# Two operand tiles moved by 160 bytes in SBUF, the tiles behind them by 512

## The chip, the cores and the metric

The kernel runs on one core of one Trainium2 chip. The metric is device time of one execution in microseconds. Engines are named as in the profile: PE is TensorE (PEld its weight loads), DVE is VectorE, ACT is ScalarE, POOL is GpSimd, SP is SyncE, from whose queue all DMAs of the kernel are issued.

## The reference

A network of three layers on 512 tokens of width 1024, in float32. Layers 0 and 1 are attention blocks (stick-breaking attention, then dilated attention), layer 2 mixes a gated linear recurrence of four heads with differential attention of four heads and is modulated by a vector computed from a condition c. Each layer ends in a gated feed-forward network of width 2816:

```python
u = rmsnorm(h, norm2_w[l]) * (1.0 + sc2) + sh2
ff = (jax.nn.silu(u @ w_ffn_gate[l]) * (u @ w_ffn_up[l])) @ w_ffn_down[l]
h = h + g2 * ff
```

Nearly all the arithmetic is products of the token matrix with weight matrices: queries, keys and values, the output products, and gate, up and down of the feed-forward networks.

## The kernel before

**Layout.** Tokens lie along the free axis, features on the 128 partitions. h, the running state, is one tile of 8 k-tiles by 512 tokens. A product needs float32 accuracy out of float32r matmuls, so each operand is split in two: xh is the operand rounded to float32r and xl the rest, both of the shape of h (ACT writes xh in `split_hi`, DVE writes xl in `split_lo`, or `out_operand` does both for the attention's output o). Weights are split the same way into whi (ACT) and wlo (DVE).

**The trio.** One 128x128 weight tile costs three matmuls of 512 columns, `mm3`: xh by whi, xl by whi, xh by wlo. The moving operand is x, the stationary one the weight tile.

```python
def mm3(o, w, x, first, last, n=T):
    E.mm(o, w[0], x[0], first, False, n=n)
    E.mm(o, w[0], x[1], False, False, n=n)
    E.mm(o, w[1], x[0], False, last, n=n)
```

`gemm_a` runs 8 k-tiles of one output tile, 24 matmuls into one PSUM bank. `gemm_wide` runs several output tiles side by side. `out_proj` runs the attention output's product in two parts. In `vcols` (the values of layer 2) the roles are turned: 128 tokens of xh or xl are stationary and four weight tiles move, whi,xh and its like in the profile. `ffn` makes the gate and up products from xh and xl, with 22 column tiles each; its two halves write the activations to eleven tiles ph0 to ph10 and their rests to pl0 to pl10, and the down product runs the same trio on these, 33 matmuls for an output tile. In the last layer the gate and up products of the first three column tiles run in two halves of 256 tokens, and so do the first tiles of the input product and the end of an output product.

**The weight stream.** The host packs all weights in the order of use (`weight_plan`). A unit of 16 tiles, 1 MB, is loaded into one of two buffers wraw; each half of it, 8 tiles, is split into one of three whi and wlo buffers of 1024 columns.

**What sets the order.** The helper class `Core` records each instruction with a planned clock for each engine; threads wait for planned times and flags, and the order of every engine's list follows from it, once, when the program is built. Addresses play no part in it.

**SBUF.** Persistent tiles are taken first, in the order h, xh, xl, vt, cr (masks and the identity), ones, eps, mod, sc, acc, acc2, rb, rc, gv (lines 395 to 408). Behind them come the pool of the weight buffers, small work tiles, and a pool for each phase. Each tile starts at a multiple of 32 bytes. In each partition they start at:

```
tile          first byte    remainder by 512    remainder by 2048
h                  16512                 128                  128
xh                 32896                 128                  128
xl                 49280                 128                  128
cr                 67264                 192                 1728
wraw               76064                 288                  288
whi (3)     92448 + 4096                 288                  288
wlo (3)    104736 + 4096                 288                  288
ph0 to ph10       129312                 288                  288
pl0 to pl10       151840                 288                  288
```

A k-tile of xh or xl, and each of the ph and pl, is 2048 bytes; a weight tile is 512 bytes, so the weight tiles of a buffer take four places by 2048.

Of the kernel before, what the change touches and what calls it, by code (L numbers as in the profile page):

```python
# [10 lines left out]
FT = mybir.dt.float32  # L11
# [6 lines left out]
P = 128  # L18
# [7 lines left out]
EPS = 1e-6  # L26
# [120 lines left out]
class Pool:  # L147
    """A tile pool that knows when the slot of a new tile is free."""
# [13 lines left out]
class Core:  # L162
    """Emission helpers. A clock per engine and the times at which data are there order the
    instructions of the threads that a phase consists of: a thread yields the time, the flag or
    the condition it waits for."""
# [24 lines left out]
    def inherit(self, name, old):  # L190
        """The tile takes over the slot of an older one."""
        t = [max(w, r) for _, _, w, r, _, _ in self.spans.pop(old, [])]
        if t:
            self.spans[name] = [(0, 1 << 30, 0.0, max(t), None, None)]
# [26 lines left out]
    def _run(self, eng, cost, outs, ins):  # L221
        """The time at which an instruction ends, and when others may use what it made."""
        t = max(getattr(self, eng), self._ready(eng, outs, ins)) + cost
        setattr(self, eng, t)
        self._done(eng, outs, ins, t + LAT)
        return t + LAT
# [69 lines left out]
    def dma(self, out, a, kb, sbuf=False):  # L296
        """sbuf: the source lies on chip."""
        self.nc.sync.dma_start(out, a)  # L298
        t = max(self.dma_t, self._ready("dma_t", [out], [a] if sbuf else []) + 1.4, self.pe_t + 1.4) + kb / 360.0
        self.dma_t = t  # L300
        self._done("dma_t", [out], [a] if sbuf else [], t + DMALAT)
        return t + DMALAT
# [4 lines left out]
    def there(self, *aps):  # L307
        """Waits until the tensor engine may use these."""
        t = self._ready("pe_t", (), aps)
        if t > self.pe_t:  # L310
            yield t

    def clear(self, *aps):
        """Waits until the tensor engine may write these."""
        t = self._ready("pe_t", aps, ())
        while t > self.pe_t:
            yield t
            t = self._ready("pe_t", aps, ())
# [22 lines left out]
    def reserve(self, banks):  # L341
        """Takes these banks out of the pool, the ones in use when they are released."""
        self.held = [b for b in banks if b not in self.free]
        self.free = [b for b in self.free if b not in banks]
# [9 lines left out]
    def run(self, main):  # L354
        """Threads run when what they wait for is there, by priority; main fills in between."""
        self.spawn(main, 1000)
        live = self.threads
        while live:
            ready = []
            for th in live:  # L360
                c = th[3]
                if c is None or (c in self.flags if isinstance(c, str) else c()):
                    ready.append(th)
            assert ready, ([(th[0], th[3]) for th in live], self.free)
            now = [th for th in ready if th[4] <= self.pe_t]
            if now:
                th = min(now, key=lambda q: (q[0], q[1]))
            else:
                th = min(ready, key=lambda q: q[4])
                self.pe_t = th[4]  # L370
            th[3], th[4] = None, 0.0
            try:
                r = next(th[2])
            except StopIteration:
                live.remove(th)
                continue
            if isinstance(r, (int, float)):
                th[4] = r
            else:
                th[3] = r  # L380
# [3 lines left out]
def kernel(ctx: ExitStack, tc, wst, wada, xT, vec, cst, rope, bias1, alibi, hmask, out):  # L384
# [10 lines left out]
    h = persist.tile([P, KT, T], FT, name="h")  # L395
    xh = persist.tile([P, KT, T], FR, name="xh")
# [11 lines left out]
    gv = persist.tile([P, 64], FT, name="gv")  # L408

# [33 lines left out]
    def finish(hu):  # L443
        """Splits a half where the engines have nothing else to do."""
        hs, ls = highs[hu], lows[hu]
        while hs or ls:
            if quiet:
                yield lambda: not quiet
                continue
            th = max(E.act_t - SLACK, E._ready("act_t", [hs[0][0]], [hs[0][1]])) if hs else 1e9  # L450
            tl = max(E.dve_t - SLACKD, ls[0][0]) if ls else 1e9
            if min(th, tl) > E.pe_t:
                yield min(th, tl)
            elif th <= E.pe_t:
                raise_(hu)
            else:
                lower(hu)

        load_ahead()
# [9 lines left out]
    def load_ahead():  # L469
        """The next unit takes the place of one whose halves are split."""  # L470
        while state["loaded"] < NUNITS:
            old = 2 * (state["loaded"] - RAWBUFS)
            if any(x >= state["prepped"] or highs[x] or lows[x] for x in range(max(old, 0), old + 2)):
                break
            load_unit()
# [79 lines left out]
    def gemm_wide(banks, i0, hook=None, need=None, wide=False, halves=None):  # L555
        """Several m-tiles side by side, while the operand is still being made; wide: their weights alternate."""
# [41 lines left out]
    def update(m, bank, tag, x=True, gain=None, scale=None, gain2=None, after=None, t=None):  # L598
        """h[m] += psum, its squares, and (x) the next product's operand; t is the half of the tokens."""
# [63 lines left out]
    def col_sums(src, bank, tbs=ALL, c0=0, first=True, s0=0):  # L663
        """Sums over the partitions; the first ones into a bank come with first set."""
        for tb in tbs:
            E.mm(ps[:, bank, c0 + tb:c0 + tb + 1], src[:, tb * P - s0:(tb + 1) * P - s0], ones, first, True, n=16,
                 group=False)
            first = False

    def newton(dst, y, m, n):  # L670
        """dst = y (1.5 - m y^2 / 2)."""
        t = tmp.tile([P, 2, n], FT, name="nw", bufs=4)
        E.stt(t[:, 0], y, -0.5, m, OP.mult, OP.mult, n=4)
        E.tt(t[:, 1], t[:, 0], y, OP.mult, n=4)
        return E.stt(dst, t[:, 1], 1.5, y, OP.add, OP.mult, n=4)
# [7 lines left out]
    def rstd_bank(dst, bank, width, tbs=ALL):  # L683
        """dst = (sums / width + EPS)^-1/2."""
# [19 lines left out]
    def norm(tag, cols, banks=None, table=None, gate=None):  # L704
        """rc and rb from acc."""
# [26 lines left out]
    def zv(g, hd, c0, c1):  # L732
        """Columns of a head's scores: two heads share the bank of group 1."""
        if g == 1:
            return ps[:, 2, hd * 256 + c0:hd * 256 + c1]
        return ps[:, ZB[g][hd], c0:c1]
# [6 lines left out]
    def make_pad(pool):  # L743
        """The stationary operands of group 1 span all rows, so that its heads may share a bank."""
# [10 lines left out]
    def split_two(t, lo, src, scale):  # L755
        """The high parts of two heads, each on its rows of t[:, hd], and the low parts."""
# [9 lines left out]
    def stacked(pool, name, src, bufs=1, scale=1.0):  # L766
        """The stationary operand of two heads: a head's high part on its rows, its low part on the others."""
# [4 lines left out]
    def doubled(pool, name, src, bufs=1, scale=1.0):  # L772
        """The moving operand of two heads: a head's high part on both halves of the rows; and the low parts."""
# [10 lines left out]
    def place(t, src, other):  # L784
        """Each head's rows of src to its own rows of t[:, hd] or to the others."""
# [20 lines left out]
    def out_operand(tag, o, flags, xfree, order=tuple(range(KT))):  # L806
        """The operand of out_proj takes the place of the phase's own, k-tile by k-tile."""
# [8 lines left out]
    def out_proj(tag, upd, order=tuple(range(KT)), scale=None, halves=None):  # L816
        """h += o @ w, in two parts: the k-tiles that come first, and the last ones."""
# [120 lines left out]
    def evac_v(tag, pool, p, bank, vz, keep=False):  # L938
        """Two heads' values: the norm's factor, then keys to the partitions; a head's stationary
        operand is its high part beside its low one."""  # L940
# [21 lines left out]
    def pv(tag, pool, p, w, vz, o, hd, own=True):  # L962
        """A head's values by its weights; own: the weights are those of this head alone."""
# [22 lines left out]
    def attention0(pool):  # L986
# [27 lines left out]
        def first_hook(k):  # L1014
            """The operands of the first product, piece by piece as the loads bring them."""
# [402 lines left out]
    def norm_in(t):  # L1418
        """The norm after layer 1 and the one before layer 2, from the sums of h^2 and (h g)^2."""
# [74 lines left out]
    def head_norm(pool, bank, width, gain, dst):  # L1494
        """dst = rmsnorm over the partition axis of the PSUM bank, times a per-partition gain."""
# [10 lines left out]
    def layer2(pool):  # L1506
# [70 lines left out]
        def vcols(dst, flag):  # L1577
            """The values of four heads, tokens on the partitions."""
# [212 lines left out]
    def scaled(t):  # L1791
        """h times the last norm's gain, once its squares are there."""
# [139 lines left out]
```

## Time and profile before

| what | value |
|---|---|
| median of 3 runs | 1958.1 us (1957.89 to 1958.9) |
| profiled execution: span from first to last instruction | 1956.9 us |
| lies around the span, median run against it | 1.2 us |
| PE busy | 1940.5 us, 99% |
| DVE busy | 1139.1 us, 58% |
| ACT busy | 843.1 us, 43% |
| HBM read | 186.26 MB, 96 GB/s over the span |

The profile is of one execution. The time of that execution is known as its span alone; the median run stands 1.2 us above it. Durations of matmuls overlap, and PE's busy time is their union; the distance between two starts is not among the page's columns and comes from start times. Line 229 is the matmul call of the helper `mm`, 235 the transposes, 242 ACT's activations, 260 and 276 DVE's tensor operations.

### The profile page before, as it was taken

The page shows a single profiled execution, that of the slowest core. Times are in us where ns is not written, and L with a number is a line of the kernel's source. Part 1 is how long each engine was busy: PE and PEld are TensorE (multiplying, and loading weights), DVE is VectorE, ACT ScalarE, POOL GpSimd, SP SyncE. Part 2 cuts the span into 40 slices and gives each one's busy share as a digit, 9 for nine tenths or more (in the row PEclk, how much of TensorE's full clock was granted, in tenths as well). Part 3 has the DMA queues.
Part 4 walks back from the last instruction along what each step waited for, and adds up shares of the span by engine and source line. Part 5 has one row for each costly group of instructions (what it writes and reads, how often), then busy time and mean ns, then how long its engine had stood idle before and what let it go on. Part 6 is the DMA issues. An engine that isn't in the chain of part 4 may idle for free.

```text
span 1956.9 us, 23731 instructions
## 1 busy us (share of the span) xinstructions
PE 1940.5 (99%) x9331; PEld 1593.4 (81%) x9331; DVE 1139.1 (58%) x1946; ACT 843.1 (43%) x1361; POOL 7.0 (0%) x14
## 2 busy tenths in 40 slices
PE   9999999999999999999999999999999999999998
PEld 6888888888778878878888888898888888888887
DVE  5877865655665578887443344474777563333334
ACT  4866743322333466665322223352546352212233
POOL 0000000000000000000000000000000000000000
PEclk9999999999999999999999999999999999999999
DMA  6333224544442344431322222222121222222221
GB/s 192 99 85 97 76 86 176 194 178 172 185 170 86 123 130 128 126 114 65 108 94 99 87 108 87 104 84 97 54 82 44 87 87 86 99 95 89 106 86 65
DMA packets 48303, 211.94 MB, mean 108 GB/s; under 512 B 7056, under 2 KB 10304, under 8 KB 29248
## 3 DMA queue, kind: packets, MB, share of 16 engines
q1 hardware_dynamic: 48192, 210.43, 31.7%
q8 instruction: 73, 1.20, 0.2%
q14 instruction: 38, 0.31, 0.0%
HBM read 186.26 MB, written 2.10 MB: 96 GB/s over the span
## 4 chain that ended last, share of the span: by engine, by line
PE 96%; DVE 2%; DMA 1%; ACT 1%; issue 0%; SPq 0%; POOLq 0%; POOL 0%; DVEq 0%; ACTq 0%
PE ps L229 94%; PE ps L235 2%; DMA wraw<-wst 0%; DVE wlo L260 0%; DMA h<-xT 0%; DVE xl L276 0%; ACT xh L242 0%; DVE ut L276 0%; SPq L298 0%; ACT whi L242 0%; DVE h L260 0%; ACT sqh L242 0%; ACT ut L242 0%; DVE h L276 0%; DVE e L276 0%
## 5 line engine op out<-in xcount | busy, mean ns | idle before, releaser
L229 PE MATMUL ps<-xh,whi 128*128 128x512 f32 (+1 forms) x1856 | 728.7, 393 | 3.5 <-ACT whi L242 2.0
L229 PE MATMUL ps<-xh,wlo 128*128 128x512 f32 (+1 forms) x1856 | 722.4, 389 | 0.5 <-DVE wlo L260 0.5
L229 PE MATMUL ps<-xl,whi 128*128 128x512 f32 (+1 forms) x1856 | 719.3, 388 | 2.1 <-POOL xl L264 1.9
L242 ACT ACTIVATE whi<-wraw 128x1024 fp32r<-128x1024 f32 (+1 forms) x280 | 290.8, 1039 | 626.3 <-PE ps L229 579.6
L260 DVE TENSOR_TENSOR wlo<-wraw,whi 128x1024 fp32r<-128x1024 f32 (+1 forms) x280 | 335.6, 1199 | 337.1 <-ACT whi L242 334.3
L229 PEld LDWEIGHTS ps<-xh,whi 128*128 128x128 f32 x1856 | 348.8, 188 | 82.0 <-ACT whi L242 3.8
L229 PEld LDWEIGHTS ps<-xl,whi 128*128 128x128 f32 x1856 | 348.9, 188 | 80.6 <-POOL xl L264 2.9
L229 PEld LDWEIGHTS ps<-xh,wlo 128*128 128x128 f32 x1856 | 348.4, 188 | 78.8 <-DVE wlo L260 1.6
L229 PE MATMUL ps<-ph,whi 128*128 128x512 f32 (+1 forms) x572 | 214.2, 374 | 0.0
L229 PE MATMUL ps<-pl,whi 128*128 128x512 f32 (+1 forms) x572 | 213.3, 373 | 0.0
L229 PE MATMUL ps<-ph,wlo 128*128 128x512 f32 (+1 forms) x572 | 213.2, 373 | 0.0
L229 PEld LDWEIGHTS ps<-ph,wlo 128*128 128x128 f32 x572 | 107.7, 188 | 19.1
L229 PEld LDWEIGHTS ps<-ph,whi 128*128 128x128 f32 x572 | 107.7, 188 | 19.0
L229 PEld LDWEIGHTS ps<-pl,whi 128*128 128x128 f32 x572 | 107.7, 188 | 18.9
L260 DVE TENSOR_TENSOR fu<-ps,rb 128x512 f32<-128x512 f32 x44 | 30.4, 690 | 102.5 <-PE ps L229 102.5
L260 DVE TENSOR_TENSOR h<-ps,h 128x512 f32<-128x512 f32 (+1 forms) x82 | 49.8, 621 | 61.9 <-PE ps L229 59.8
L242 ACT ACTIVATE fs<-fg 128x512 f32<-128x512 f32 x44 | 27.8, 631 | 91.0 <-DVE fg L260 91.0
L260 DVE TENSOR_TENSOR fs<-ps,fs 128x512 f32<-128x512 f32 x22 | 15.2, 692 | 73.7 <-PE ps L229 73.0
L242 ACT ACTIVATE ph<-fs 128x512 fp32r<-128x512 f32 x66 | 41.8, 633 | 28.8 <-DVE fs L260 28.8
L276 DVE SCALAR_TENSOR_TENSOR adacc<-adaw,sc,adacc 128x1024 f32<-128x1024 f32 x42 | 53.7, 1279 | 0.0
L242 ACT ACTIVATE e<-e 128x1024 f32<-128x1024 f32 (+1 forms) x48 | 41.3, 905 | 21.7 <-DVE e L269 21.6
L242 ACT ACTIVATE s<-s,md 128x256 f32<-128x256 f32 (+3 forms) x80 | 45.9, 585 | 9.8 <-DVE md L269 8.4
(211 smaller groups left out, 1977.6 us busy)
## 6 DMA issues: line engine op xcount, KB each, us to landing
wraw<-wst SPq DMA_DIRECT2D x148, 1024.0 KB, 4.7
adaw<-wada SPq DMA_DIRECT2D x48, 512.0 KB, 5.7
qhh<-hin SPq DMA_DIRECT2D x32, 128.0 KB, 2.4
rfs<-rf SPq DMA_DIRECT2D x64, 64.0 KB, 2.0
khh<-rf SPq DMA_DIRECT2D x32, 128.0 KB, 2.5
h<-xT SPq DMA_DIRECT2D x8, 256.0 KB, 4.9
kst<-hin SPq DMA_DIRECT2D x16, 128.0 KB, 2.4
kst<-qkf SPq DMA_DIRECT2D x16, 128.0 KB, 2.4
```

The source lines that it names most:

```text
L229: self.nc.tensor.matmul(out, lhsT, rhs, start=start, stop=stop, skip_group_check=not group)
L235: self.nc.tensor.transpose(out, in_, ident)
L242: self.nc.scalar.activation(out, in_, func, **kw)
L260: self.nc.vector.tensor_tensor(out, a, b, op)
L276: self.nc.vector.scalar_tensor_tensor(out, a, s, b, op0, op1)
```

## The change

Two tiles that nothing reads or writes are put among the persistent ones, one of 40 floats (160 bytes) ahead of xh and one of 88 floats (352 bytes) behind gv. The diff also drops comments and docstrings, which leave empty lines.

```diff
     h = persist.tile([P, KT, T], FT, name="h")
+    persist.tile([P, 40], FT, name="gap0")
     xh = persist.tile([P, KT, T], FR, name="xh")
     xl = persist.tile([P, KT, T], FR, name="xl")
     vt = persist.tile([P, NVEC], FT, name="vt")
...
     gv = persist.tile([P, 64], FT, name="gv")
+    persist.tile([P, 88], FT, name="gap1")
```

h stays where it is. xh, xl and the persistent tiles behind them move by 160 bytes, all pools by 512:

```
tile          first byte    remainder by 512    remainder by 2048
h                  16512                 128                  128
xh                 33056                 288                  288
xl                 49440                 288                  288
cr                 67424                 352                 1888
whi (3)     92960 + 4096                 288                  800
wlo (3)    105248 + 4096                 288                  800
ph0 to ph10       129824                 288                  800
pl0 to pl10       152352                 288                  800
```

The instructions of every engine, and the DMAs, stand in the same order as before, each with the same shapes.

## Rows read from the trace of the kernel before

**Rows 1.** The page: span, PE's busy time, granted clock by slices, chain by line.

```profile
span 1956.9 us, 23731 instructions
PE 1940.5 (99%) x9331; PEld 1593.4 (81%) x9331; DVE 1139.1 (58%) x1946; ACT 843.1 (43%) x1361; POOL 7.0 (0%) x14
...
PEclk9999999999999999999999999999999999999999
...
PE ps L229 94%; PE ps L235 2%; DMA wraw<-wst 0%; DVE wlo L260 0%; DMA h<-xT 0%; DVE xl L276 0%; ACT xh L242 0%; DVE ut L276 0%; SPq L298 0%; ACT whi L242 0%; DVE h L260 0%; ACT sqh L242 0%; ACT ut L242 0%; DVE h L276 0%; DVE e L276 0%
```

**Rows 2.** Waits: who waited for whom, us in total, times, longest.

```profile
ACT whi L242 <- PE ps L229: 585.2, 194, 7.2
```

**Rows 3.** Groups by shape: busy us, mean ns | idle before.

```profile
L229 PE MATMUL ps<-xh,whi 128*128 128x512 f32 x1728 | 691.3, 400 | 3.4 <-ACT whi L242 2.0 <-DVE o L260 0.9 <-DVE h L260 0.5
L229 PE MATMUL ps<-xh,wlo 128*128 128x512 f32 x1728 | 686.4, 397 | 0.5 <-DVE wlo L260 0.5
L229 PE MATMUL ps<-xl,whi 128*128 128x512 f32 x1728 | 682.4, 395 | 0.0
```

**Rows 4.** Tile xh, 1105:1222 and 1765:1884: count, durations, first to last start.

```profile
L229 PE MATMUL ps<-xh,wlo x168: 399/399/399, 1104.6 to 1221.5; 128*128 128x512 f32 x168
...
L229 PE MATMUL ps<-xh,wlo x171: 399/399/399, 1764.6 to 1883.6; 128*128 128x512 f32 x171
```

**Rows 5.** Tile ph, 1045:1099 and 1704:1760, the same columns.

```profile
L229 PE MATMUL ps<-ph,whi x80: 389/389/389, 1044.8 to 1098.5; 128*128 128x512 f32 x80
...
L229 PE MATMUL ps<-ph,wlo x83: 389/389/389, 1704.0 to 1759.8; 128*128 128x512 f32 x83
```

**Rows 6.** Stretches: length, then busy us of PE, PEld, DVE, ACT, POOL; clock, DMA.

```profile
700.00:960.00 260.00, 259.12 (x1253) 208.51 (x1252) 202.06 (x526) 161.85 (x367) 0.00 (x0) 1.00 0.37 110
1702.00:1761.00 59.00, 59.00 (x262) 48.84 (x261) 19.52 (x20) 11.72 (x12) 0.00 (x0) 1.00 0.25 91
1765.00:1884.00 119.00, 119.00 (x512) 95.73 (x511) 38.65 (x41) 33.14 (x42) 0.00 (x0) 1.00 0.27 97
```

**Rows 7.** Tile whi, 1313:1319.6, where whi moves.

```profile
L229 PE MATMUL ps<-whi,xh x9: 392/397/400, 1313.0 to 1318.6; 128*128 128x512 f32 x9
```

**Rows 8.** Groups by shape: whi moving.

```profile
L229 PE MATMUL ps<-whi,xh 128*128 128x512 f32 x64 | 26.3, 410 | 0.0
```

**Rows 9.** Timeline of PE, xh to ph: start, duration, instruction.

```profile
1222.44 0.40 PE L229 MATMUL ps<-ph,whi 128*128 128x512 f32 x1
...
1224.29 0.39 PE L229 MATMUL ps<-ph,wlo 128*128 128x512 f32 x1
```

**Rows 10.** Timeline of PE, ph to xh.

```profile
1099.23 0.40 PE L229 MATMUL ps<-xh,whi 128*128 128x512 f32 x1
...
1099.69 0.40 PE L229 MATMUL ps<-xh,wlo 128*128 128x512 f32 x1
1099.93 0.40 PE L229 MATMUL ps<-xh,whi 128*128 128x512 f32 x1
...
1101.10 0.40 PE L229 MATMUL ps<-xh,wlo 128*128 128x512 f32 x1
```

**Rows 11.** Groups by shape: 256 columns.

```profile
L229 PE MATMUL ps<-xh,whi 128*128 128x256 f32 x128 | 37.4, 293 | 0.2
...
L229 PE MATMUL ps<-ph,whi 128*128 128x256 f32 x88 | 25.4, 289 | 0.0
```

**Rows 12.** Groups by shape: the largest on cr.

```profile
L235 PE MATMUL ps<-cr,s 128*128 128x128 f32 x200 | 26.5, 272 | 0.0
```

**Rows 13.** Groups by shape: DVE's second parts.

```profile
L260 DVE TENSOR_TENSOR pl<-fs,ph 128x512 fp32r<-128x512 f32 x66 | 45.2, 685 | 1.4 <-ACT ph L242 1.4
...
L260 DVE TENSOR_TENSOR xl<-o,xh 128x512 fp32r<-128x512 f32 x24 | 16.0, 684 | 2.4 <-ACT xh L242 2.4
```

**Rows 14.** DMA issues: count, KB each, us to landing.

```profile
wraw<-wst SPq DMA_DIRECT2D x148, 1024.0 KB, 4.7
```

**Rows 15.** Groups by shape: the split of a half.

```profile
L260 DVE TENSOR_TENSOR wlo<-wraw,whi 128x1024 fp32r<-128x1024 f32 x272 | 332.2, 1222 | 336.9 <-ACT whi L242 334.1 <-PE ps L229 1.0
```

## The prediction

> **What bounds the kernel.** I read the page first, then the chain of waits, the list of waits, the costliest groups with their shapes kept apart, and last the start times of single matmuls. The page says that TensorE (PE) is busy for 1940.5 of the 1956.9 us, at a granted clock of 9 tenths or more in every slice, and that the chain which ended last lies for 94% of the span on one line, PE's matmul call [rows 1]. The list of waits says which way the dependence runs: ACT, which splits the weights into whi, waited 585.2 us in 194 places for PE to give a weight buffer back [rows 2]. So weights lie ready and PE takes them at its own pace. Other engines can only matter where they hold PE up, and PE's idle time before its largest groups is 3.4, 0.5 and 0.0 us [rows 3]. The time is therefore the sum of the distances from one matmul's start to the next.
>
> A busy PE is not PE at its peak, because the listed durations overlap. They say 390 to 400 ns for a matmul that starts every 230 ns or so, hence durations are no price here; start times are. Where a group runs without a break, the first and the last start with the count between them give the distance. In the second half of layer 1's gate and up products, xh,wlo starts at 1104.6 and for the 168th time at 1221.5: 116.9 / 167 = **0.700 us per weight tile**, which is three matmuls (xh by whi, xl by whi, xh by wlo). The last layer's gate and up products give 119.0 / 170 = 0.700 [rows 4]. The down products run the same three matmuls, 512 columns each, on the tiles ph and pl: 53.7 / 79 = 0.680 in layer 1 and 55.8 / 82 = **0.680** in the last one [rows 5]. Shape, type, clock and weight buffers are the same, and yet a tile of weights costs 20 ns less.
>
> What could be the difference? Not other engines at work: in 1765 to 1884, where the trio costs 0.700, DVE is busy 38.65 of 119 us (32%) and DMA's share is 0.27; in 1702 to 1761, where it costs 0.680, DVE is busy 19.52 of 59 (33%) and DMA's share is 0.25 [rows 6]. Not waits either: no idle time stands before these groups. What does differ is where the two operands of a matmul lie. The table of starts above gives xh and xl a remainder of 128 by 512, and whi, wlo, ph and pl one of 288. While one matmul streams its moving operand, PE already loads the next stationary one, so both are read at once: xh against whi at remainders 160 apart, ph against whi at equal ones. A third pairing speaks for the distance between the two, rather than for the place of the moving one: where whi moves and xh is stationary (the values of layer 2), nine whi,xh start between 1313.0 and 1318.6, 5.6 / 8 = 0.700 again [rows 7], although whi as a moving operand has the 288 that ph has.
>
> **The change, part by part.** No instruction is added, removed or put elsewhere; each engine's list is the same, DMAs included, and so are the queues.
>
> *xh and xl, 160 bytes further.* Their remainder becomes 128 + 160 = 288, that of the weights is 288 before and after, so each xh or xl matmul then pairs with its weights as ph does today, at equal remainders by 512 and in the same four places by 2048. The price of a trio in a long run should go from 0.700 to 0.680, 20 ns less. There are 1728 trios of 512 columns [rows 3] and 64 with whi moving [rows 8]. In full that is 1792 x 0.020 = 35.8 us, the upper bound.
>
> It isn't all had, since the short distance sets in late. When layer 1's down product follows on the gate and up products, the first eight ph and pl starts after 1222.44 take 1.85 us, 0.231 each [rows 9], and only then do they come at 0.227. The first eight xh and xl starts after the other changeover, at 1099.23, take 1.87 us, 0.234 each [rows 10]. So the first eight of a run gain about 2.5 ns each, 20 ns in all, and those behind them 6.7. By the weight plan 3 x 352 - 24 = 1032 of the trios are gate and up products in runs of hundreds: 1032 x 0.020 = 20.6 us. The other 760 belong to the attention phases, the input product of layer 2 and the output products, mostly in runs of eight k-tiles, that is 24 matmuls: 8 x 2.5 + 16 x 6.7 = 127 of 160 ns, or 0.8 of the full price: 760 x 0.020 x 0.8 = 12.2 us. Were all of those runs as short as eight matmuls, 760 x 0.0075 = 5.7 us would be left. I take 20.6 + 12.2 = **32.8 us**, between 26.3 and 35.8.
>
> *The 128 trios of 256 columns.* At this width xh,whi takes 293 ns and ph,whi 289 [rows 11]; these are durations, and I take zero, with three times that difference as both ends: 128 x 0.012 = 1.5 us either way.
>
> *The small persistent tiles, 160 bytes further; the pools, 512.* The pools keep their remainders among themselves. Against them move cr (masks and identity), ones, rb, acc. cr is the largest user among them: 200 transposes of 128 columns [rows 12], and products with sph and spl in layer 0. If each transpose gained or lost what one of the three does above, 6.7 ns, that is 200 x 0.0067 = 1.3 us; as much again for the others gives 2.6 us either way. Whether the new distance suits them no row tells, so I take zero and keep both ends.
>
> *DVE and ACT on the moved tiles.* DVE's xl from o and xh reads operands at different remainders and takes 684 ns; pl from fs and ph reads equal ones and takes 685 [rows 13]. So zero for these, on either side of the change.
>
> *What is late next.* PE asks for weights 3% sooner. A unit of 1 MB lands 4.7 us after its issue [rows 14] and lasts 16 x 0.70 = 11.2 us now, 10.9 then; DVE needs 1.22 us for a half's wlo [rows 15] and a half lasts 5.44 us. The phase where others come nearest to PE is layer 1's attention, 700 to 960, with DVE at 202 of 260 us [rows 6]; its 3% can be covered. I book nothing and let a rival carry it.
>
> The sum: 1956.9 - 32.8 = 1924.1 us for the profiled span. The median of the runs is 1958.1, 1.2 us above this span, so 1958.1 - 32.8 = 1925.3, given as **1925 us**. With both uncertain prices (1.5 + 2.6) on top of the bounds this case lies in 1918 to 1936.
>
> **The rivals.** *It belongs to the role, not to the address: 1958 us.* Every run of xh is slow and every long run of ph is fast, in all phases, so anything that tells xh from ph would do as well: xl lies 16384 bytes behind xh and pl 22528 behind ph, a bank is summed over 24 matmuls or over 33, and neither is touched by the change. For it: no trio of the trace has xh at any other remainder. Against it: the whi,xh matmuls have another order and other roles and still cost 0.700. [...] Chance 0.09.
>
> *Equal remainders harm xh: about 1994 us, slower.* The 160 bytes may be what keeps the two reads apart, and ph may be quick for something else. The longest distances in the rows are 0.24 (1099.69 to 1099.93, [rows 10]); a trio of three such would cost 0.72, 20 ns more, 1792 x 0.020 = 36 us. It decides as soon as a long run of xh stands above 0.700. Against it: ph at equal remainders with the same buffers. Chance 0.04.
>
> *PE gets faster and attention doesn't follow: 1937 us.* If DVE and ACT set the pace in the attention phases, only the gate and up products gain: 1958.1 - 20.6 = 1937.5. Against it stands the small idle time of PE now. Chance 0.07.
>
> That the change doesn't move what it says can't be: the starts are fixed when the program is built, and they stand above.
>
> **How the numbers follow.** The forecast has 0.80. With the third rival, faster by over 0.2% (3.9 us, about what a measurement of this kernel tells from no change) has 0.87; no change has 0.09 and slower 0.04. The range for 8 in 10 is the forecast's own, 1918 to 1936, stretched to 1940 to take in the third rival: it leaves out the two with 0.13 together and a little of the tails.
>
> **What would show it.** Right: runs of xh at 0.680 per trio in the gate and up products, unchanged 0.680 on ph, no new idle time on PE, about 21 us gone from the three feed-forward phases and 12 from the rest; whi,xh at 0.680 too. Wrong: 0.700 in the gate and up products (role), more than that (harm), or 0.680 with idle time of PE before matmuls of the attention phases (others set the pace).

## The result and the profile after

The changed kernel takes 1928.5 us (median of 4 runs, 1928.12 to 1929.18) against 1958.0 before; the ratio is 0.9848, 95% interval 0.9834 to 0.9862. That is 29.5 us less, where 32.8 were forecast, and inside the range of 1918 to 1940. The profiled span went from 1956.9 to 1926.3 us, 30.6 less, at a granted clock of 0.998 before and 0.999 after. Two single executions of the experiments below, 3914.9 us (xl and wlo off) and 2365.6 us (xl alone off), stood far above the others of their kernels, and the times given for these two leave them out.

First the page of the kernel after, its span and its busy time, then the wait that showed before that weights lie ready.

```profile
span 1926.3 us, 23731 instructions
## 1 busy us (share of the span) xinstructions
PE 1909.9 (99%) x9331; PEld 1593.4 (83%) x9331; DVE 1138.1 (59%) x1946; ACT 842.6 (44%) x1361; POOL 7.0 (0%) x14
```

```profile
ACT whi L242 <- PE ps L229: 563.7, 192, 7.2
```

The same instructions ran in as many records. PE's busy time fell by 30.6 us, DVE's by 1.0 and ACT's by 0.5, and ACT still waits 563.7 us for PE to give buffers back [rows 2 had 585.2]: PE stayed the bound, and PE alone got faster.

Now the starts. These are the tiles xh, xh, ph and whi in four stretches of the kernel after: the gate and up products of layer 1 and of the last layer, the down product of layer 1, and the stretch where whi moves. The columns are count, durations, first to last start.

```profile
L229 PE MATMUL ps<-xh,wlo x169: 389/389/389, 1087.7 to 1202.0; 128*128 128x512 f32 x169
```

```profile
L229 PE MATMUL ps<-xh,wlo x162: 389/389/389, 1739.9 to 1849.3; 128*128 128x512 f32 x162
```

```profile
L229 PE MATMUL ps<-ph,whi x82: 389/389/389, 1026.8 to 1081.8; 128*128 128x512 f32 x82
```

```profile
L229 PE MATMUL ps<-whi,xh x9: 389/389/389, 1292.6 to 1298.0; 128*128 128x512 f32 x9
```

114.3 / 168 and 109.4 / 161 give 0.680 us per trio of xh, where [rows 4] had 0.700; ph keeps its 0.680 (55.0 / 81 = 0.679, [rows 5]); whi moving over xh comes at 5.4 / 8 = 0.675, by ends that are good to 0.1 us, where [rows 7] had 0.700. The listed durations, between 392 and 399 ns in layer 1's stretch before, are 389 now, ph's number.

The changeover from xh to ph, on PE's timeline after, answers to [rows 9]:

```profile
1202.21 0.39 PE L229 MATMUL ps<-ph,whi 128*128 128x512 f32 x1
...
1204.02 0.39 PE L229 MATMUL ps<-ph,wlo 128*128 128x512 f32 x1
```

Eight starts now take 1.81 us, 0.226 each, where they took 1.85. The slow beginning of a run of ph was itself a matter of distance: coming from xh, which now is in step too (at the same remainder as the weights), ph is quick from its first matmul.

Where were the 30.6 us had? One stretch of each kind, from a matmul to the same matmul, before and after. The gate and up products of layer 1's second half run from 1099.23 [rows 10] to 1222.44 [rows 9] before, 123.21 us, and from 1082.53 to 1202.21 after:

```profile
1082.53 0.39 PE L229 MATMUL ps<-xh,whi 128*128 128x512 f32 x1
...
1202.21 0.39 PE L229 MATMUL ps<-ph,whi 128*128 128x512 f32 x1
```

That is 119.68 us, 3.53 less. The groups by shape of that stretch after give the count, 176 of each of the three:

```profile
L229 PE MATMUL ps<-xh,whi 128*128 128x512 f32 x176 | 68.5, 389 | 0.0
```

So each trio gained 20.1 ns, the full price. The attention of layer 1 before, and then after, between the same two matmuls:

```profile
700.07 0.39 PE L229 MATMUL ps<-xl,whi 128*128 128x512 f32 x1
...
960.01 0.40 PE L229 MATMUL ps<-xh,wlo 128*128 128x512 f32 x1
```

```profile
689.20 0.40 PE L229 MATMUL ps<-xl,whi 128*128 128x512 f32 x1
...
945.62 0.39 PE L229 MATMUL ps<-xh,wlo 128*128 128x512 f32 x1
```

259.94 us became 256.42, again 3.52 less, but for 270 trios, as the groups by shape of that stretch before have them:

```profile
L229 PE MATMUL ps<-xh,wlo 128*128 128x512 f32 x270 | 107.0, 396 | 0.0
```

Put on these trios alone that is 13.0 ns for each, or 0.65 of the full price.

### The profile page after: what moved, and what is told of

The parts are those of the page before. It is cut to its first block, busy times and chain, and to the rows that moved or that the text cites. A ratio compares the mean times of both kernels' runs of the same rounds, so it can differ in the third digit from the quotient of the medians.

```text
span 1926.3 us, 23731 instructions
## 1 busy us (share of the span) xinstructions
PE 1909.9 (99%) x9331; PEld 1593.4 (83%) x9331; DVE 1138.1 (59%) x1946; ACT 842.6 (44%) x1361; POOL 7.0 (0%) x14
## 4 chain that ended last, share of the span: by engine, by line
PE 96%; DVE 2%; DMA 1%; ACT 1%; issue 0%; SPq 0%; POOLq 0%; POOL 0%; DVEq 0%; ACTq 0%
PE ps L229 94%; PE ps L235 2%; DMA wraw<-wst 0%; DMA h<-xT 0%; DVE wlo L260 0%; DVE xl L276 0%; ACT xh L242 0%; DVE ut L276 0%; SPq L298 0%; ACT whi L242 0%; DVE h L260 0%; ACT sqh L242 0%; ACT ut L242 0%; DVE h L276 0%; DVE e L276 0%
## 5 line engine op out<-in xcount | busy, mean ns | idle before, releaser
L229 PE MATMUL ps<-xl,whi 128*128 128x512 f32 (+1 forms) x1856 | 711.4, 383 | 2.2 <-POOL xl L264 1.9
L229 PE MATMUL ps<-xh,wlo 128*128 128x512 f32 (+1 forms) x1856 | 710.8, 383 | 0.5 <-DVE wlo L260 0.5
L260 DVE TENSOR_TENSOR fs<-ps,fs 128x512 f32<-128x512 f32 x22 | 15.2, 692 | 70.2 <-PE ps L229 69.5
```

The costliest lines, as they stand in the source:

```text
L229: self.nc.tensor.matmul(out, lhsT, rhs, start=start, stop=stop, skip_group_check=not group)
L260: self.nc.vector.tensor_tensor(out, a, b, op)
```

## The experiments

Theory 1 says that the distance between the moving operand and the weights sets the price of a trio; theory 2 says that it is the place of xh. In this section "by 256" is the remainder after division by 256 bytes, and "off" a distance that isn't 0.

**Move all together.** Only the first gap is put in.

```diff
+    persist.tile([P, 40], FT, name="gap0")
     xh = persist.tile([P, KT, T], FR, name="xh")
```

> Only the first gap of the change: xh, xl and everything behind them move by 160 bytes together. xh then lies at remainder 288 by 512, as in the change, and the weights at 448, so the two stay 160 apart as before. Theory 1 (the distance between the moving operand and the weights by 512 sets the price): trio of xh in long runs 0.700 us, no gain, 1958 us. Theory 2 (the place of xh itself sets it): 0.680 and about 1928 us. Theory 3 (something else in the change, such as small tiles) has no price for it.

1959.6 us against 1959.6 before on that chip, ratio 0.9999 (0.9989 to 1.0008). Tile xh in layer 1's gate and up products:

```profile
L229 PE MATMUL ps<-xh,wlo x129: 399/399/399, 1105.8 to 1195.4; 128*128 128x512 f32 x129
```

89.6 / 128 = 0.700. xh lay where the change puts it, and nothing was gained. Theory 2 falls.

**Move the weights instead.** Only the second gap.

```diff
     gv = persist.tile([P, 64], FT, name="gv")
+    persist.tile([P, 88], FT, name="gap1")
```

> Only the second gap of the change: xh and xl stay where they were, at remainder 128, and all pools move by 352 bytes, so the weights lie at 128 as well. Theory 1 (distance): trio of xh 0.680 us, about 1928 us, though neither operand lies where it does in the change. Theory 2 (place of xh): 0.700 and 1958 us. If both count, something between.

1928.5 us, ratio 0.9843 (0.9829 to 0.9858), the whole gain of the change with xh left alone. Tile xh, the same stretch:

```profile
L229 PE MATMUL ps<-xh,wlo x133: 389/389/389, 1106.1 to 1195.9; 128*128 128x512 f32 x133
```

89.8 / 132 = 0.680. Neither operand lies where the change has it, but their distance is that of the change. Theory 1 stands. All pools move with the weights here; the last experiment puts wlo alone out of line.

**By 512 or by 256?** xh and xl lie 256 bytes further than in the change.

```diff
-    persist.tile([P, 40], FT, name="gap0")
+    persist.tile([P, 104], FT, name="gap0")
...
-    persist.tile([P, 88], FT, name="gap1")
+    persist.tile([P, 24], FT, name="gap1")
```

> xh and xl 256 bytes beyond the change, so that their distance to the weights is 256 by 512. If distance counts by 256, as the probe with ph at 256 says, xh's trio is 0.680 us and the kernel takes about 1928 us; if it counts by 512 or more, and the probe showed something of ph alone, 0.700 and 1958 us.

1927.8 us, ratio 0.9844 (0.9827 to 0.9860). Tile xh:

```profile
L229 PE MATMUL ps<-xh,wlo x133: 389/389/389, 1105.7 to 1195.4; 128*128 128x512 f32 x133
```

89.7 / 132 = 0.680. A distance of 256 was as good as 0, which the change has (0.680).

**The price of other distances.** The down products served as a probe, in kernels that otherwise are the one after: a gap at the head of each feed-forward pool moves ph and pl against the weights, by another amount in each layer, and xh stays in step. Each of these kernels was executed once. Distances that aren't multiples of 32 were had with an offset of 1 or 4 elements into one large tile.

```diff
+        pool.tile([P, {"F0": 8, "F1": 16, "F2": 32}[tag]], FT, name="gapf")
         ph = [pool.tile([P, T], FR, name=f"ph{i}") for i in range(HALF)]
```

> The kernel after with the feed-forward pools moved against the weights by 32 bytes in layer 0, 64 in layer 1 and 128 in layer 2, so that ph and pl, which were at distance 0, show the price of these distances in the down products. Theory 1: the trio of ph and pl leaves 0.680 us for 0.700 at one or more of these distances, with xh unchanged at 0.680. Theory 2 and the theory of roles: 0.680 in all three.

> As the first probe, with ph and pl 96, 192 and 256 bytes off in layers 0, 1 and 2. The prices found so far are 0, 20/3, 40/3 or 20 ns per trio. If only the lowest bits of the distance count, 96 costs what 32 does (20 ns), 192 what 64 does (6.7) and 256 what 128 does (20).

> ph and pl 160, 224 and 16 bytes off in layers 0, 1 and 2; xh as in the change. If distance counts by 256, 160 is the old distance of whi as moving tile to xh and costs 20 ns per trio, and 224 is 32 bytes short of a full step, 20 ns or less. 16 bytes are half the step between two tiles: if one line of SBUF serves both reads, it costs nothing; otherwise it may go either way, also below 0.680.

> ph and pl 4, 144 and 240 bytes off in layers 0, 1 and 2, to look for a distance cheaper than 0. So far 0 and 256 cost nothing over 0.680 us, 64 costs 6.7 ns, 16 costs 15 and the others 20 to 23. If both reads being in step is what is cheap, 4 bytes cost little or nothing (one element), 144 some 20 ns, and 240, which is 16 short of a full step, about what 16 does, 15 ns. A trio under 0.680 anywhere would mean that distance 0 still has a collision in it.

Tile ph of the first of these, in the down products of layers 0, 1 and 2 (32, 64 and 128 bytes):

```profile
L229 PE MATMUL ps<-ph,whi x51: 393/394/397, 411.6 to 446.6; 128*128 128x512 f32 x51
```

```profile
L229 PE MATMUL ps<-ph,whi x79: 394/394/394, 1030.8 to 1084.3; 128*128 128x512 f32 x79
```

```profile
L229 PE MATMUL ps<-ph,whi x75: 392/392/398, 1685.9 to 1737.7; 128*128 128x512 f32 x75
```

Of the second, layers 0, 1 and 2 (96, 192 and 256 bytes); of the third, layer 2 (16 bytes); of the last, layers 0 and 2 (4 and 240 bytes):

```profile
L229 PE MATMUL ps<-ph,whi x51: 392/392/392, 411.9 to 446.9; 128*128 128x512 f32 x51
```

```profile
L229 PE MATMUL ps<-ph,whi x78: 394/394/394, 1031.1 to 1085.0; 128*128 128x512 f32 x78
```

```profile
L229 PE MATMUL ps<-ph,whi x77: 389/389/389, 1686.2 to 1737.9; 128*128 128x512 f32 x77
```

```profile
L229 PE MATMUL ps<-ph,whi x75: 390/397/398, 1685.9 to 1737.4; 128*128 128x512 f32 x75
```

```profile
L229 PE MATMUL ps<-ph,whi x50: 398/401/403, 411.9 to 446.9; 128*128 128x512 f32 x50
```

```profile
L229 PE MATMUL ps<-ph,whi x75: 396/396/396, 1686.2 to 1738.0; 128*128 128x512 f32 x75
```

Worked out as everywhere, first to last start over the count less one, all thirteen:

| distance of ph, pl to the weights, bytes | us per trio |
|---|---|
| 0 (the kernel after), 256 | 0.679, 0.680 |
| 64 | 0.686 |
| 16 | 0.696 |
| 32, 96, 128, 144, 192, 224, 240 | 0.700 |
| 160 | 0.702 |
| 4 | 0.714 |

The old distance of xh, 160 below the weights, is 96 by 256, and cost the 0.700 that 96 costs here. The ends are listed to 0.1 us, which leaves about 2 ns of a trio open; the starts in the traces to the nanosecond give 0.687 for 64, 0.695 for 16 and 0.703 for 160. So the price follows the distance with other tiles in another product as well. None of the distances tried is cheaper than 0. Two guesses of the expectations fell: that a small step out of line is cheap (4 bytes is the dearest of all), and that only the lowest bits count (192 costs what 96 does, not what 64 does). Nor is the price the same on both sides of a full step: 16 costs 15 or 16 ns, 240 costs 20. At 4, 16, 144 and 240 bytes the tiles also start off a multiple of 32, as in no other run, so for these four the distance and the place of the tile itself aren't told apart.

**One of the two tiles off.** xl alone is put at the old distance (the second gap between xh and xl, none behind gv):

```diff
     xh = persist.tile([P, KT, T], FR, name="xh")
+    persist.tile([P, 88], FT, name="gapm")
     xl = persist.tile([P, KT, T], FR, name="xl")
```

> xh at the distance of the change, xl alone at the old distance (160 bytes apart by 512 from the weights). Theory 1, with each matmul paying for itself: one of three matmuls is slow, a trio costs 0.680 + 0.007 = 0.687 us, the kernel about 1938 us. If what counts is the place of xh against xl: 0.700, 1958 us. If the loss of one matmul delays the two behind it: up to 0.700.

1948.7 us, ratio 0.9942 (0.9926 to 0.9959). Tile xh:

```profile
L229 PE MATMUL ps<-xh,wlo x131: 390/390/390, 1105.7 to 1195.8; 128*128 128x512 f32 x131
```

90.1 / 130 = 0.693: one matmul in three is off and 13 ns of 20 are lost. That is more than the share of one matmul in three, 6.7 ns. The probe repeats this with ph and pl:

> Only one of the two tiles off: in layer 0 ph by 96 bytes with pl in step, in layer 1 pl by 96 with ph in step, in layer 2 pl by 160. If the price follows from distances alone, whatever the tiles, layer 1 repeats xl off by 160 bytes downwards (which is 96 by 256): 13.3 ns per trio; layer 2 repeats xl off by 96 downwards (160 by 256): 16.6 ns; layer 0, with two of the three matmuls off, costs between 13 and 20 ns. If each off matmul paid 6.7 ns on its own: 6.7, 6.7 and 13.3 ns for layers 1, 2 and 0.

Tile ph in layers 0 (ph off by 96), 1 (pl by 96) and 2 (pl by 160); the other of the two tiles lies 256 bytes from the weights' remainder, in step:

```profile
L229 PE MATMUL ps<-ph,whi x51: 394/396/396, 411.6 to 446.4; 128*128 128x512 f32 x51
```

```profile
L229 PE MATMUL ps<-ph,whi x79: 397/397/397, 1030.8 to 1084.9; 128*128 128x512 f32 x79
```

```profile
L229 PE MATMUL ps<-ph,whi x75: 397/397/397, 1686.2 to 1737.8; 128*128 128x512 f32 x75
```

34.8 / 50 = 0.696, 54.1 / 78 = 0.694 and 51.6 / 74 = 0.697. Layer 1 was to repeat the 0.693 of xl and does; layer 2 was to repeat the run below, and does. So in these two cases the same distances gave the same price with other tiles.

**Its own weights or the next ones?** While a matmul streams, the weights of the next are loaded: in the kernel after, xl by whi starts at 1109.96, the load of wlo runs from 1109.96 to 1110.15, and xh by wlo starts at 1110.18. Three kernels put xl, or wlo, or both 96 bytes below the rest. xl comes ahead of xh for this, and wlo ahead of whi. The diff is that of both. xl alone has only its first part; wlo alone has the second and the third, with a gap of 24 ahead of xl and none between xl and xh, which keeps both in step:

```diff
-    persist.tile([P, 40], FT, name="gap0")
-    xh = persist.tile([P, KT, T], FR, name="xh")
     xl = persist.tile([P, KT, T], FR, name="xl")
+    persist.tile([P, 24], FT, name="gapm")
+    xh = persist.tile([P, KT, T], FR, name="xh")
...
-    persist.tile([P, 88], FT, name="gap1")
+    persist.tile([P, 64], FT, name="gap1")
...
-        hi = wpool.tile([P, 1024], FR, name="whi", bufs=3)
         lo = wpool.tile([P, 1024], FR, name="wlo", bufs=3)
+        if hu == 0:
+            wpool.tile([P, 24], FT, name="gapw")
+        hi = wpool.tile([P, 1024], FR, name="whi", bufs=3)
```

> xh and whi at one remainder by 512, xl and wlo 96 bytes below it, at another. While xh by whi streams, whi is loaded for the next matmul; while xl streams, wlo is loaded; while xh by wlo streams, the next whi is loaded. Theory 1a (a matmul pays for the distance between its moving operand and the weights loaded for the next one): all pairs at distance 0, trio 0.680 us, xh products as quick as in the change. Theory 1b (it pays for the distance to its own weights): xl by whi and xh by wlo are off, trio 0.693 us or more. The down products have wlo off against pl and own ph: slower under both.

> xl alone 96 bytes off, xh, whi and wlo at one remainder. Both theories: one pair of the trio off, 0.687 to 0.693 us; the down products stay at 0.680. It is the measure for the run before it: 96 bytes must cost something here.

> wlo alone 96 bytes off, xh, xl and whi at one remainder. Theory 1a: the pair of xl streaming and wlo loading is off, the same price as with xl alone off. Theory 1b: the pair xh by wlo is off, a like price; but then the run with both off must add the two.

Both off: 1959.6 us, ratio 1.0005 (0.9993 to 1.0017). xl alone: 1951.5, 0.9959 (0.9945 to 0.9974). wlo alone: 1966.3, 1.0039 (1.0020 to 1.0059), which is slower than before, since the down products have wlo off as well. Tile xh of each, in that order, in layer 1's gate and up products; the fourth row is tile ph of the last kernel:

```profile
L229 PE MATMUL ps<-xh,wlo x130: 390/393/395, 1105.8 to 1195.5; 128*128 128x512 f32 x130
```

```profile
L229 PE MATMUL ps<-xh,wlo x130: 390/394/397, 1106.0 to 1195.9; 128*128 128x512 f32 x130
```

```profile
L229 PE MATMUL ps<-xh,wlo x129: 392/392/396, 1106.0 to 1195.6; 128*128 128x512 f32 x129
```

```profile
L229 PE MATMUL ps<-ph,wlo x58: 392/392/396, 1043.7 to 1083.6; 128*128 128x512 f32 x58
```

89.7 / 129 = 0.695, 89.9 / 129 = 0.697, 89.6 / 128 = 0.700, and 39.9 / 57 = 0.700. Theory 1a (the next weights) wanted 0.680 for both off, and falls in this form. Theory 1b (its own weights) wanted the two prices to add, 17 and 20 ns, and both together cost 15: it falls too, as far as prices add. A price with a ceiling isn't ruled out, since xh and xl both off, as before the change, cost no more than wlo alone, 20 ns. Which weights count, a matmul's own or the next ones, stays open, and no run shows a mechanism: that two reads meet, as the forecast and the expectations have it, is the author's conjecture.

## Why the prediction was right, and where it was short

- *What bounds the kernel*: right. PE's busy time took the whole fall, and PE's idle time before its largest group is 3.3 us, as against 3.4 in [rows 3]:

```profile
L229 PE MATMUL ps<-xh,whi 128*128 128x512 f32 x1728 | 684.9, 396 | 3.3 <-ACT whi L242 1.8 <-DVE o L260 0.9 <-DVE h L260 0.5
```

- *The difference between 0.700 and 0.680 is the distance of moving operand and weights*: right, and now shown by moving both (nothing), either (all) and ph (the loss). The forecast argued it by 512; at a distance of 256 the trio took 0.680 too, which the rows before couldn't tell.
- *The gate and up products, 20.6 us*: right for an unbroken run, a little high in all. The stretch measured gives 20.1 ns per trio for a forecast of 20. PE's matmuls stand in the same order in both traces, so their starts can be compared one by one: all 1032 trios gained 19.6 us, 19.0 ns each, since three of the six halves have other matmuls between theirs.
- *The other 760 trios, 12.2 us, taken as 0.8 of the full price*: mis-sized, and the main reason why the forecast was high. Compared one by one they gained 10.3 us or 0.68 of 15.2, all other matmuls together 0.6, and the attention of layer 1 alone gave 0.65. The step that was off is the run of 24 matmuls. Trios stand between matmuls of other shapes more than that, as here in layer 1's attention before:

```profile
724.07 0.40 PE L229 MATMUL ps<-wl,vz 128*128 128x512 f32 x1
724.30 0.40 PE L229 MATMUL ps<-xh,whi 128*128 128x512 f32 x1
724.54 0.39 PE L229 MATMUL ps<-xl,whi 128*128 128x512 f32 x1
724.77 0.39 PE L229 MATMUL ps<-xh,wlo 128*128 128x512 f32 x1
725.00 0.27 PE L235 MATMUL ps<-cr,vT 128*128 128x128 f32 x1
```

Of 170 unbroken runs of xh and xl at 512 columns, gate and up products among them, 137 are shorter than 24 matmuls and 97 have nine or fewer; the 376 trios in the 137 gained 11.7 ns each. The bounds of this term, 5.7 and 15.2, held it.

- *The first eight of a run gain 2.5 ns each, as ph's do behind xh*: near in size, 2.8 ns measured over all runs, and 5.7 for the sixteen behind them where 6.7 were taken. Behind xh in step, ph shows no slow beginning in the kernel after (0.226 from the first start, 0.231 before); it went with the distance too.
- *The median 1.2 us above the profiled span*: it is 2.2 after. Of the 3.3 us by which the medians fell short of the forecast, 2.2 lie in the spans and 1.1 in which executions were profiled: where an execution's time and span are both on record, they are 1.8 us apart before and after.
- *256 columns, the small tiles, DVE and ACT at zero*: nothing speaks against it; compared one by one, the starts of these 128 trios gained less than 0.1 us in all. xh,whi at 256 columns had 293 ns and has 293 (first row below), the transposes by cr 272 and 272 (second row, groups by shape after).

```profile
L229 PE MATMUL ps<-xh,whi 128*128 128x256 f32 x128 | 37.5, 293 | 0.2
```

```profile
L235 PE MATMUL ps<-cr,s 128*128 128x128 f32 x200 | 26.5, 272 | 0.0
```

- *The rivals*: that it belongs to the role fell with the weights moved alone: with the same instructions in the same order the trio took 0.680 or 0.700 us by where the weights lay, with the pools around them. That equal remainders harm xh fell at once. That attention doesn't follow fell as a whole, with 0.65 of the price had there.

## What to carry to other kernels

Where matmuls follow each other without a gap, compare the distance of starts for every pair of operand tiles, not the durations; two groups of one shape whose starts lie at different distances can be a sign that addresses matter, as 0.700 against 0.680 us per trio was here. For float32r products of 512 columns that load new weights each time, put the moving tiles and the weight tiles at the same remainder by 256 bytes: two unused tiles, 512 bytes together in each partition, were worth 1.5% here (1958.0 to 1928.5 us). A new small tile ahead of a large operand can take that away unseen, as the one ahead of xl did with about two thirds of it (1948.7 us), so such remainders are to be written down as a condition of the layout.

## What the runs showed of the hardware

- PE's pace in this kernel's float32r matmuls of 512 columns with new weights each time went with the byte distance of moving operand and weights in SBUF, the same at 0 and 256 bytes: 0.680 us per trio there, 0.686 at 64, 0.700 to 0.702 at 32, 96, 128, 160, 192 and 224. The 0.714 at 4 bytes is of a tile that also starts off a multiple of 32.
- With both moving tiles off by a multiple of 32 a trio lost 7 ns at 64 bytes and 20 to 23 at the others tried. With one tile off by 96 or 160 it lost 13 or 17 (xl, pl), 17 (ph) and 20 (wlo).
- Even in step, a matmul of 512 columns started every 0.680 / 3 = 0.227 us; no distance tried brought less.
